# Gates of the last dense tile: from one-hot matmuls to scatters that add into cleared DRAM

## The chip, the cores and the metric

The kernel runs on one core of one Trainium2 chip. The metric is the time of one execution in microseconds (us) on the device; runs of the kernel before took 4015.42 to 4017.12 us, with a median of 4016.08 over 3 runs. A profile of one further execution comes with them.

## The reference, cut to what matters

The model is a backbone of two layers over 256 context tokens and 512 latent tokens of width 1024. Each layer has a mixer (layer 0: attention and a short convolution; layer 1: mLSTM) and then PEER, a mixture of 16384 tiny experts. For each token and each of 8 heads, PEER scores two sets of 128 keys, takes the best 16 of each, the best 16 of their sums, and a softmax over these:

```
cand = (s1[..., :, None] + s2[..., None, :]).reshape(PEER_BLOCK, PEER_HEADS, PEER_TOPK * PEER_TOPK)
cidx = (i1[..., :, None] * PEER_NKEYS + i2[..., None, :]).reshape(...)
top, pos = lax.top_k(cand, PEER_TOPK)
idx = jnp.take_along_axis(cidx, pos, axis=-1)
g = jax.nn.softmax(top, axis=-1)
ue, ve = u[idx], v[idx]
act = jax.nn.gelu(jnp.einsum('td,thkd->thk', xb, ue).astype(jnp.float32), approximate=False)
return jnp.einsum('thk,thkd->td', (g * act).astype(xb.dtype), ve)
```

So each token has 128 pairs of an expert's number and a gate. Two heads of one token can pick the same expert; their gates then add up. Layer 0 does this for 768 tokens (6 tiles of 128), layer 1 for the 512 latent ones (4 tiles).

## The kernel before, in words

PEER has two phases a layer. `peer_u` (L659) computes the activations of the experts, `peer_v0` (L1091) and `peer_v1` (L1151) multiply them by the gates and by v. Tokens are treated in two ways. The first `NG` tiles (2 in layer 0, 1 in layer 1) are *gathered*: GpSimd fetches the u rows of the chosen experts by indirect DMA, 128 rows of 4 KB each time (`dot`, L917), and VectorE takes the dot product (L923). All other tiles (4 and 3) are *dense*: TensorE multiplies them with all 16384 rows of u, in a loop of 128 steps c, each with 24 matmuls (8 blocks of the width, 3 products of the split float32, L676) over 512 columns in layer 0 and 384 in layer 1. A step's result goes through Gelu on ScalarE (`ga`, L1022) and to DRAM. Before each step ScalarE and VectorE split the next block of u into a high and a low part (`split_u`, uh and ul, with high priority). In steps 0 to 16 TensorE also projects the queries and VectorE takes the top 16 of the keys.

A dense tile needs its gates as a matrix over all experts and tokens. `stage2(t)` makes it. `cands`, `decode` and `soft` find the 128 expert numbers (two halves, idk) and gates of each token, for four heads at a time, on VectorE. `tr` transposes them on TensorE, `fin` makes 16-bit copies. Then, for every 8 tokens, `prep` (L857 to L860) makes one-hot matrices with 4 VectorE operations, and two `gbuild` (L874, L876) multiply them, 8 matmuls into one PSUM bank (gps), which ScalarE copies into `stg`. After 32 tokens four stores of 512 KB each (L756) put `stg` into the DRAM tile `gd`, laid out as [4, 128, 128, 32]: group of 32 tokens, first key, second key, token. The v phase loads it with `gf` (L1062).

What of this is done in which step is set by a planner at the end of `peer_u`. It has queues of items with a cost in us and the earliest step: `route` (heads of the gathered tiles), `one` (heads, prep and gbuild of the dense tiles), `dots` and `bgq` (modulation weights of the next layer). Each step is given a share (`given`) of the sum of all costs, in the ratio of its slack, and takes items from the queue that lies furthest behind its line (`lag`), which runs from the first to the second step in `goal`, until the share is spent. Instructions on one engine run in the order in which they stand in its queue, and so do the DMAs that SP, ScalarE and GpSimd issue. A DMA that depends on an earlier one waits on the issuing engine.

The first mixer (`mixer0`) loops over 8 heads of attention in units; the scores of a head run beside the weighted sum of the head before it.

Of the kernel before, what the change touches and what calls it, by code (L numbers as in the profile page):

```python
# [10 lines left out]
F32 = mybir.dt.float32  # L11
# [3 lines left out]
U32 = mybir.dt.uint32  # L15
AF = mybir.ActivationFunctionType
ALU = mybir.AluOpType
# [4 lines left out]
P = 128  # L22
# [23 lines left out]
TOPK = 16  # L46
# [14 lines left out]
GAB = 4  # L61

NG = (2, 1)
SEGS = ((0, NCTX), (NCTX, NLAT))


# [5 lines left out]
def kernel(ctx: ExitStack, tc: tile.TileContext, a: dict, out: bass.AP, dbg=None, stop=None):  # L72
    nc = tc.nc
# [6 lines left out]
    def mkpsum(st, name):  # L80
# [5 lines left out]
    tok = [a["tok"][t * P:(t + 1) * P, :] for t in range(NT)]  # L86
    gds = [[dram.tile([4, P, P, 32], F32, name=f"gd{v}_{t}") for t in range(n - NG[v])]
           for v, n in enumerate((NT, NLAT // P))]

    cv = const.tile([P, KD, 2], F32, name="cv")  # L90
    nc.sync.dma_start(cv, a["cvec"])
# [4 lines left out]
    ng = const.tile([P, 2, 2, KD], F32, name="ng")  # L96
# [118 lines left out]
    def mixer0(pk_open):  # L215
        with ExitStack() as st:
            rst = ExitStack()
            mcp = mkpool(st, "m0mc")
            mch = mcp.tile([P, 4, T], F32R, name="mch")
            mcl = mcp.tile([P, 4, T], F32R, name="mcl")  # L220
            m0b = mkpool(rst, "m0b", side="right")
            pqh = m0b.tile([P, 2, T], F32R, name="pqh")
# [234 lines left out]
            with ExitStack() as st2:  # L457
# [62 lines left out]
                for h in range(H0 + 1):  # L520
                    pts = {}
                    sc = scores(qks.pop(h), pts) if h < H0 else []
                    for u in range(8):
                        if u < len(sc):
                            sc[u]()
                        if u < len(prev):
                            prev[u]()
                        if u == 1 and 2 <= h + 1 < H0:
                            qks[h + 1] = prep(h + 1)
                    prev = attend(h, pts)  # L530
# [120 lines left out]
    def peer_u(layer, tiles):  # L651
# [8 lines left out]
        with ExitStack() as s1:  # L660
# [27 lines left out]
            pool.iota(c15, pattern=[[0, 4 * TOPK]], base=15, channel_multiplier=0)  # L688
            prev1 = up.tile([P, 4, TOPK + 1], F16, name="prev1", bufs=1)
            vec.memset(prev1, 0.0)  # L690
            urow = [up.tile([P, P], U32, name=f"urow{j}", bufs=1) for j in range(ng)]
            gact = [up.tile([P, P], F32, name=f"gact{j}", bufs=1) for j in range(ng)]
            sq = ExitStack()
# [67 lines left out]

            def stage2(t):
                H = 2 if t < ng else 4
                keep = t >= ng
                d = {}

                def cands(h0):
                    def f():
                        if h0 == 0:
                            d["g"] = up.tile([P, PH, TOPK], F32, name="g" if keep else f"g{t}", bufs=2 if keep else 1)  # L770
                            if keep:
                                d["id"] = up.tile([P, 2, PH, TOPK], F32, name="idk")
                        hs = slice(h0, h0 + H)
                        top = d["top"] = up.tile([P, H, TOPK], F32, name="top")
                        pos = d["pos"] = up.tile([P, H, TOPK], U32, name="pos")
                        vv = v16[t].rearrange("p (h q) k -> p h q k", q=2)[:, hs]
                        c = up.tile([P, H, 65], F32, name="cand", bufs=1)
                        for o, r0, rn, m in ((0, 0, 1, 16), (16, 1, 2, 8), (32, 3, 4, 4), (48, 7, 8, 2), (64, 15, 1, 1)):
                            vec.tensor_tensor(c[:, :, o:o + rn * m].rearrange("p h (r m) -> p h r m", m=m),
                                              vv[:, :, 0, r0:r0 + rn, None].to_broadcast([P, H, rn, m]),  # L780
                                              vv[:, :, 1, None, 0:m].to_broadcast([P, H, rn, m]), op=ALU.add)
                        for h in range(H):
                            w_ = up.tile([P, 65], F32, name="candw", bufs=1)
                            topk16(top[:, h, :], pos[:, h, :], c[:, h, :], w_)
                    return f

                def decode(h0):
                    def f():
# [12 lines left out]
                        vec.tensor_tensor(pt, ps_, pt, op=ALU.bitwise_and)  # L801
                        vec.tensor_copy(pq[:, 1], pt.rearrange("p (h k) -> p h k", k=TOPK))
                        if not keep:
                            d["t"] = up.tile([P, 2, H, TOPK], F32, name="idt")
                        dst = d["id"][:, :, h0:h0 + H] if keep else d["t"]
                        for q, (tab, op) in enumerate(((lo16, ALU.is_ge), (i16v, ALU.is_equal))):
                            eq = up.tile([P, H, TOPK, TOPK], F16, name="eq", bufs=1)
# [19 lines left out]
                def ids(h0):  # L827
                    ks = slice(h0 * TOPK, (h0 + H) * TOPK)
                    return ks, [d["t"][:, q].rearrange("p h k -> p (h k)") for q in range(2)]

                def tr():
                    tp = pp.tile([P, 512], F32, name="tp", bufs=2)
# [65 lines left out]

                def heads(h0):
                    need = 2 * (h0 + H) + 1  # L900
                    last = None if keep else rows(h0)
                    return [(cands(h0), 1.6 * H, need), (decode(h0), 0.7 + 1.4 * H, need), (soft(h0), 1.0, need)] + \
                        ([(last, 0.5, need)] if last else [])

# [38 lines left out]
                GP.extend((gp, io))  # L943

            qi = [q_items(hp) for hp in range(2 * PH)]
            st2 = [stage2(t) for t in range(n)]
            route = []
            for h0 in range(0, PH, 2):
                route += [x for t in range(ng) for x in st2[t][0](h0)] + [(found, 0.0, 0)]
            heads = [[x for h0 in (0, 4) for x in st2[t][0](h0)] + [(st2[t][1], 0.0, 0)] for t in range(ng, n)]  # L950
            one = heads[0]
            for t in range(ng, n):
                nxt = heads[t + 1 - ng] if t + 1 < n else []
                one.append((st2[t][2], 1.0, 0))
                for pf, g0, g1 in st2[t][3]:
                    one.append((pf, 2.75, 2 * PH + 1))
                    for gf in (g0, g1):
                        pend.append(gf)
                        if len(pend) > 3:
                            one.append((pend.pop(0), 0.0, 0))  # L960
                        if nxt:
                            one.append(nxt.pop(0))
                one += nxt
# [1 line left out]
            total_dots = P * ng  # L965
            dots = [(dot(x), 1.3, (x, 1)) for x in range(total_dots)] + [(st2[t][4], 0.3, (total_dots - 1, 1)) for t in range(ng)]
            bgq = [(f, 1.33 * (2 if layer == 0 and x < 24 else 1), 0) for x, f in enumerate(bg)]
            queues = [route, one, dots, bgq]
            goal = [(4, 18), (8, 118), (8, 125), (17, 124)]
            whole = [sum(x[1] for x in q) for q in queues]  # L970
            left = list(whole)
            slack = []
# [12 lines left out]
            def can(q, c):  # L985
                if not queues[q]:
                    return False
                need = queues[q][0][2]
                return need[0] < at["rows"] if isinstance(need, tuple) else need <= c or c == 127

            uhl, los = {}, {}

# [17 lines left out]
            for c in range(128):  # L1010
# [26 lines left out]
                while True:  # L1037
                    ok = [q for q in range(len(queues)) if can(q, c)]
                    if not ok or (spent > given and c < 127):
                        break  # L1040
                    q = max(ok, key=lambda q: lag(q, c))
                    f, w, _ = queues[q].pop(0)
                    with tc.issue_after(los[min(c + LAG, 127)]):
                        f()
                    left[q] -= w
                    spent += w
                if 1 <= c <= 2 * PH:
                    for f in qi[c - 1][3]:
                        f()
# [620 lines left out]
```

## Time and profile before

The profiled execution took 4018.06 us; its span from the first instruction to the last is 4015.8 us.

| engine | busy us | share of the span |
|---|---|---|
| TensorE, matmuls (PE) | 3754.6 | 93% |
| TensorE, weight loads (PEld) | 3208.5 | 80% |
| VectorE (DVE) | 3220.2 | 80% |
| ScalarE (ACT) | 1512.0 | 38% |
| GpSimd (POOL) | 1317.5 | 33% |

The DMA engines moved 1036.51 MB, 258 GB/s on the mean. The mean granted clock of TensorE is 0.970 of full speed.

A busy time is a sum over instructions that can overlap: a matmul's record lasts longer than the distance to the next. A wait is put down to what ended it. In the rows below, a number after x is a count, and what stands in brackets at a row's end is the idle time of that engine before it and what ended it. SPq and ACTq are the queues in which these engines issue DMAs. The DMA share is the mean busy share of the core's 16 DMA engines and can read above 1.

### The profile page before, as it was taken

The page shows a single profiled execution, that of the slowest core. Times are in us where ns is not written, and L with a number is a line of the kernel's source. Part 1 is how long each engine was busy: PE and PEld are TensorE (multiplying, and loading weights), DVE is VectorE, ACT ScalarE, POOL GpSimd, SP SyncE. Part 2 cuts the span into 40 slices and gives each one's busy share as a digit, 9 for nine tenths or more (in the row PEclk, how much of TensorE's full clock was granted, in tenths as well). Part 3 has the DMA queues.
Part 4 walks back from the last instruction along what each step waited for, and adds up shares of the span by engine and source line. Part 5 has one row for each costly group of instructions (what it writes and reads, how often), then busy time and mean ns, then how long its engine had stood idle before and what let it go on. Part 6 is the DMA issues. An engine that isn't in the chain of part 4 may idle for free. (4 is left out here: it accounts for less than half of the span.)

```text
span 4015.8 us, 54004 instructions
## 1 busy us (share of the span) xinstructions
PE 3754.6 (93%) x19201; PEld 3208.5 (80%) x19201; DVE 3220.2 (80%) x6734; ACT 1512.0 (38%) x2435; POOL 1317.5 (33%) x962
## 2 busy tenths in 40 slices
PE   6988989999999995999999899888999999899998
PEld 5776777877787774888888789867899999788887
DVE  7766699898899986988898854458897977588887
ACT  4355422333333332322222355542344443333333
POOL 2521201044434434767676312212012312232221
PEclk9999999999999997999999989989999999999999
DMA  7301443289899999999999721046368888899995
GB/s 244 103 6 50 159 154 130 100 307 342 303 351 333 371 366 357 389 390 388 391 388 390 266 70 44 18 170 219 107 226 291 313 294 301 316 387 360 359 357 213
DMA packets 411662, 1036.51 MB, mean 258 GB/s; under 512 B 35584, under 2 KB 170240, under 8 KB 411392
## 3 DMA queue, kind: packets, MB, share of 16 engines
q1 hardware_dynamic: 261920, 498.69, 35.7%
q0 software_dynamic: 114336, 416.34, 28.4%
q10 hardware_dynamic: 35136, 118.05, 7.5%
q8 instruction: 150, 2.46, 0.2%
q14 instruction: 120, 0.98, 0.1%
HBM read 906.05 MB, written 126.88 MB: 257 GB/s over the span
## 5 line engine op out<-in xcount | busy, mean ns | idle before, releaser
L917 POOL DMA_INDIRECT urows<-in_u_rows,urow x384 | 493.0, 1284 | 1243.6 <-DVE urows L923 847.6
L1080 POOL DMA_INDIRECT vrows<-in_v_t,vrow x384 | 601.8, 1567 | 581.0 <-DVE accg L1088 333.9
L676 PE MATMUL aps<-pnh,uh 128*128 128x512 f32 (+1 forms) x2048 | 766.0, 374 | 10.8 <-ACT ga L1022 7.1
L676 PE MATMUL aps<-pnh,ul 128*128 128x512 f32 (+1 forms) x2048 | 759.3, 371 | 2.9 <-DVE ul L111 2.9
L676 PE MATMUL aps<-pnl,uh 128*128 128x512 f32 (+1 forms) x2048 | 757.5, 370 | 0.0
L108 ACT CAST uh<-uf 128x1024 fp32r<-128x1024 f32 x256 | 269.2, 1052 | 725.9 <-PE aps L676 684.7
L923 DVE SCALAR_TENSOR_TENSOR urows<-urows,px 128x1024 f32<-128x1024 f32 x384 | 465.0, 1220 | 47.9 <-DMA urows<-in_u_rows,urow 46.8
L108 ACT CAST vh<-vf 128x1024 fp32r<-128x1024 f32 x256 | 269.2, 1052 | 552.5 <-issue 283.9
L676 PEld LDWEIGHTS aps<-pnh,uh 128*128 128x128 f32 x2048 | 389.9, 190 | 57.0 <-ACT ga L1022 9.6
L111 DVE TENSOR_TENSOR vl<-vf,vh 128x1024 fp32r<-128x1024 f32 x256 | 313.1, 1223 | 150.3 <-ACT vh L108 147.2
L676 PEld LDWEIGHTS aps<-pnh,ul 128*128 128x128 f32 x2048 | 387.9, 189 | 49.7 <-DVE ul L111 6.3
L676 PEld LDWEIGHTS aps<-pnl,uh 128*128 128x128 f32 x2048 | 388.8, 190 | 42.6
L111 DVE TENSOR_TENSOR ul<-uf,uh 128x1024 fp32r<-128x1024 f32 x256 | 312.7, 1222 | 102.9 <-ACT uh L108 100.6
L1111 PE MATMUL acc<-vh,vwh 128*128 128x512 f32 x1024 | 317.7, 392 | 48.4 <-ACT vwh L108 48.3
L1111 PE MATMUL acc<-vh,vwl 128*128 128x512 f32 x1024 | 316.8, 391 | 1.0 <-DVE vwl L111 1.0
L1111 PE MATMUL acc<-vl,vwh 128*128 128x512 f32 x1024 | 316.5, 390 | 0.0
L1088 DVE SCALAR_TENSOR_TENSOR vacc<-vrows,gw,vacc 128x1024 f32<-128x1024 f32 x254 | 314.3, 1281 | 0.0
L1111 PEld LDWEIGHTS acc<-vh,vwh 128*128 128x128 f32 x1024 | 193.2, 189 | 90.1 <-ACT vwh L108 50.1
L1176 PE MATMUL acc<-vh,vwh 128*128 128x512 f32 x768 | 238.4, 392 | 13.5 <-ACT vwh L108 12.9
L108 ACT CAST vwh<-gaf 128x512 fp32r<-128x512 f32 (+1 forms) x256 | 144.3, 564 | 277.5 <-DVE gaf L1069 178.5
L874 PE MATMUL gps<-p,p 128*128 128x128 f16 x1792 | 243.0, 296 | 4.9 <-DVE p L860 4.9
L1176 PE MATMUL acc<-vl,vwh 128*128 128x512 f32 x768 | 237.7, 391 | 0.0
(438 smaller groups left out, 7497.1 us busy)
## 6 DMA issues: line engine op xcount, KB each, us to landing
uf<-in_u_t SPq DMA_DIRECT2D x256, 512.0 KB
vf<-in_v_t SPq DMA_DIRECT2D x256, 512.0 KB
gd<-stg ACTq DMA_DIRECT2D x112, 512.0 KB
gf<-gd SPq DMA_DIRECT2D x224, 256.0 KB
wmt<-in_w_modT SPq DMA_DIRECT2D x90, 512.0 KB
gad<-ga ACTq DMA_DIRECT2D x64, 512.0 KB
gaf<-gad SPq DMA_DIRECT2D x64, 512.0 KB
gad<-ga ACTq DMA_DIRECT2D x64, 384.0 KB
```

The costliest lines, as they stand in the source:

```text
L108: act.copy(hi, src)
L111: return el.tensor_tensor(lo, src, hi.bitcast(F32), op=ALU.subtract)
L676: pe.matmul(ps[:, o:o + w], x[:, k, :], blk[q][:, k, :w], start=(k == 0 and x is wh and q == 0), stop=(k == KD - 1 and x is wl))
L874: pe.matmul(gp[:, i * P:(i + 1) * P], p1[:, g, :, i], p2[q][:, g, :, i], start=q == 0, stop=q == 1)
L917: nc.gpsimd.indirect_dma_start(out=r, out_offset=None, in_=a["u_rows"], in_offset=bass.IndirectOffsetOnAxis(ap=urow[j][:, k:k + 1], axis=0))
L923: vec.scalar_tensor_tensor(r, r, 1.0, PK["x"][j], op0=ALU.mult, op1=ALU.mult, accum_out=gact[j][:, k:k + 1])
L1080: nc.gpsimd.indirect_dma_start(out=r, out_offset=None, in_=a["v_t"].rearrange("l c k d -> (l c k) d"), in_offset=bass.IndirectOffsetOnAxis ...
L1088: vec.scalar_tensor_tensor(acc, r, gw[:, k:k + 1], acc, op0=ALU.mult, op1=ALU.add)
L1111: pe.matmul(acc[i][hf], x[:, ts_], y[:, hf * 512:(hf + 1) * 512], start=(c == 0 and first), stop=(c == 127 and end))
L1176: pe.matmul(acc[i][hf], x[:, ts_], y[:, hf * 512:(hf + 1) * 512], start=(c == 0 and first), stop=(c == 127 and last))
```

## The change

The last tile of each layer (`NSC = (1, 1)`) keeps its heads, but its gates no longer go through transposes, one-hot matrices, matmuls and stores. Instead its part of `gd` is cleared by 16 DMAs of 512 KB from a tile of zeros, one in each unit of the first mixer's attention from the second head on (32 for both layers, on SP's queue). `spots` turns each token's expert numbers into positions in `gd`, in `srow`, by two VectorE operations for each half of the heads. `scatter` then writes one column of `srow`: an indirect DMA on GpSimd's queue that adds 128 gates, one of each token and 4 bytes each, to 128 places in `gd`. There are 128 of them in a layer. They are sent between the items of the planner, after items with a cost above 1.0 us, along a line from step 8 to step 122; what is left goes out in step 125. The heads of the scattered tile get a queue of their own, `early`, with the steps 8 to 22 as its line, and the line of `one` begins at step 10 in place of 8. Three small tiles get three buffers.

```diff
+NSC = (1, 1)
+SC_END = 123
...
+    def clear(v, t, zero, x, n):
+        g = gds[v][t].rearrange("b p j t -> (b p j t)").rearrange("(x p y t) -> x p y t", x=n, p=P, t=P)
+        nc.sync.dma_start(g[x], zero[:, None, :].to_broadcast([P, P // n, P]))
...
+            zero = mcp.tile([P, P], F32, name="zero")
+            vec.memset(zero, 0.0)
+            wipe = [(v, len(gds[v]) - 1 - i, zero, x, 16) for v in range(2) for i in range(NSC[v]) for x in range(16)]
...
+                        if wipe and h:
+                            clear(*wipe.pop(0))
...
+            spos = up.tile([P, 1], F32, name="spos", bufs=1)
+            pu = up.tile([P, 2], U32, name="spu", bufs=1)
+            pool.iota(pu, pattern=[[0, 2]], base=0, channel_multiplier=1)
+            pf2 = up.tile([P, 2], F32, name="spf", bufs=1)
+            vec.tensor_scalar(pu[:, 0:1], pu[:, 0:1], 5, None, op0=ALU.logical_shift_right)
+            vec.tensor_scalar(pu[:, 1:2], pu[:, 1:2], 31, None, op0=ALU.bitwise_and)
+            vec.tensor_copy(pf2, pu)
+            vec.scalar_tensor_tensor(spos, pf2[:, 0:1], float(P * P * 32), pf2[:, 1:2], op0=ALU.mult, op1=ALU.add)
+            scat = list(range(n - NSC[layer], n))
+            srow = {t: up.tile([P, P], U32, name=f"srow{t}", bufs=1) for t in scat}
...
-                keep = t >= ng
+                keep = ng <= t < n - NSC[layer]
...
+                def spots(h0):
+                    def f():
+                        ks, (i0, i1) = ids(h0)
+                        rf = up.tile([P, 4 * TOPK], F32, name="rowf", bufs=1)
+                        vec.tensor_scalar(rf, i0, float(P * 32), spos[:, 0:1], op0=ALU.mult, op1=ALU.add)
+                        vec.scalar_tensor_tensor(srow[t][:, ks], i1, 32.0, rf, op0=ALU.mult, op1=ALU.add)
+                        gates[t] = d["g"].rearrange("p h k -> p (h k)")
+                        ready[t] += range(ks.start, ks.stop)
+                    return f
...
-                    last = None if keep else rows(h0)
+                    last = None if keep else rows(h0) if t < ng else spots(h0)
...
-            heads = [[x for h0 in (0, 4) for x in st2[t][0](h0)] + [(st2[t][1], 0.0, 0)] for t in range(ng, n)]
+            heads = [[x for h0 in (0, 4) for x in st2[t][0](h0)] + [(st2[t][1], 0.0, 0)] for t in range(ng, scat[0])]
+            early = [x for h0 in (0, 4) for t in scat for x in st2[t][0](h0)]
...
-            queues = [route, one, dots, bgq]
-            goal = [(4, 18), (8, 118), (8, 125), (17, 124)]
+            queues = [route, one, dots, bgq, early]
+            goal = [(4, 18), (10, 118), (8, 125), (17, 124), (8, 22)]
...
+            sent, due = 0, P * len(scat)
+
+            def scatter():
+                ts_ = [t for t in scat if ready[t]]
+                if not ts_:
+                    return 0
+                t = max(ts_, key=lambda x: len(ready[x]))
+                k = ready[t].pop(0)
+                nc.gpsimd.indirect_dma_start(
+                    out=gd[t - ng].rearrange("b p j (t o) -> (b p j t) o", o=1),
+                    out_offset=bass.IndirectOffsetOnAxis(ap=srow[t][:, k:k + 1], axis=0),
+                    in_=gates[t][:, k:k + 1], in_offset=None, compute_op=ALU.add)
+                return 1
...
+                    if w > 1.0 and sent * (SC_END - 9) < due * (c - 8):
+                        sent += scatter()
+                while c == 125 and scatter():
+                    sent += 1
```

## Rows read from the trace of the kernel before

**Rows 1.** Busy us of each engine by stretch; then granted clock, DMA share, GB/s.
```profile
475.00:760.00 285.00, 264.27 (x1389) 226.51 (x1390) 260.04 (x1140) 90.60 (x132) 15.71 (x13) 0.94 0.41 136
1100.00:1550.00 450.00, 440.27 (x2230) 348.75 (x2228) 409.36 (x728) 158.60 (x226) 181.44 (x136) 1.00 0.94 351
1600.00:2200.00 600.00, 600.00 (x2649) 496.94 (x2648) 533.30 (x558) 175.94 (x218) 412.00 (x229) 1.00 1.05 389
3010.00:3445.00 435.00, 435.00 (x2708) 425.69 (x2708) 347.32 (x580) 175.70 (x264) 111.78 (x91) 1.00 0.85 298
200.00:350.00 150.00, 133.42 (x732) 104.58 (x730) 111.12 (x245) 87.69 (x188) 42.86 (x27) 0.98 0.01 4
```

**Rows 2.** Groups by line, shapes apart: busy us, mean ns, idle time before.
```profile
L874 PE MATMUL gps<-p,p 128*128 128x128 f16 x1792 | 243.0, 296 | 4.9 <-DVE p L860 4.9
L860 DVE TENSOR_TENSOR p<-p2e,idT 128x1024 f16<-128x1024 f16 x224 | 148.3, 686 | 65.7 <-PE gps L874 63.7 <-PE aps L676 1.4 <-issue 0.6
L812 DVE TENSOR_REDUCE idk<-eq 128x64 f32<-128x1024 f16 x28 | 34.0, 1215 | 0.0
```

**Rows 3.** Chain of waits in layer 1: start, us, what.
```profile
3065.94 1.90 PE gps L874 x16
3067.84 4.25 PE aps L676 x24
```

**Rows 4.** TensorE in order of time, layer 0: start, us, instruction.
```profile
1517.80 1.82 PE L874 MATMUL gps<-p,p 128*128 128x128 f16 x14
1519.37 0.49 PE L676 MATMUL aps<-pnh,ul 128*128 128x512 f32 x1
```

**Rows 5.** The end of a layer's u phase, engines in order of time.
```profile
1593.75 1.22 PE L1111 MATMUL acc<-vh,vwh 128*128 128x512 f32 x2 [43.65 <-ACT vwh L108]
...
1575.21 1.22 DVE L923 SCALAR_TENSOR_TENSOR urows<-urows,px 128x1024 f32<-128x1024 f32 x1
...
1577.18 6.02 SPq L1062 DMA_DIRECT2D gf<-gd  x4
...
3452.31 0.38 SPq L1062 DMA_DIRECT2D gf<-gd  x1
```

**Rows 6.** A small VectorE operation like those added, in order of time.
```profile
1108.42 0.34 DVE L891 TENSOR_SCALAR rowf<-idt 128x32 f32<-128x32 f32 x1
```

**Rows 7.** DMA queues in 800 to 1500, then 1560 to 2200: packets, MB, share.
```profile
q10 hardware_dynamic: 15163, 55.23, 19.9%
...
q1 hardware_dynamic: 86273, 121.56, 53.9%
```

**Rows 8.** The next loads in SP's queue after the middle of attention.
```profile
368.39 10.45 SPq L579 DMA_DIRECT2D oht<-in_tok  x6
```

**Rows 9.** Gathers of u rows (L917) alone: GpSimd busy us, clock, DMA share.
```profile
760.00:1550.00 790.00, 315.46 (x239) 0.99 0.90 328
```

**Rows 10.** Gelu of steps 9 and 125: layer 0, then layer 1.
```profile
656.86 0.59 ACT L1022 ACTIVATE ga<-aps 128x512 f32<-128x512 f32 x1
1537.73 0.59 ACT L1022 ACTIVATE ga<-aps 128x512 f32<-128x512 f32 x1
2816.64 0.48 ACT L1022 ACTIVATE ga<-aps 128x384 f32<-128x384 f32 x1
3455.40 0.86 ACT L1022 ACTIVATE ga<-aps 128x384 f32<-128x384 f32 x2
```

**Rows 11.** Two gathers as issued, and the dots that waited for them.
```profile
2758.33 1.01 POOL L917 DMA_INDIRECT urows<-in_u_rows,urow  x1 [76.82 <-DVE rowf L891]
2762.81 1.27 DVE L923 SCALAR_TENSOR_TENSOR urows<-urows,px 128x1024 f32<-128x1024 f32 x1 [0.84 <-DMA urows<-in_u_rows,urow]
...
1551.77 1.98 POOL L917 DMA_INDIRECT urows<-in_u_rows,urow  x1 [0.30 <-issue]
1564.01 1.23 DVE L923 SCALAR_TENSOR_TENSOR urows<-urows,px 128x1024 f32<-128x1024 f32 x1 [1.76 <-DMA urows<-in_u_rows,urow]
```

**Rows 12.** Waits by line: us in total, times, longest.
```profile
DVE urows L923 <- DMA urows<-in_u_rows,urow: 46.8, 36, 3.4
```

More of the change, by code (lines that the diff above doesn't have):

```diff
@@ L773, in f @@
                         hs = slice(h0, h0 + H)
-                        top = d["top"] = up.tile([P, H, TOPK], F32, name="top")
-                        pos = d["pos"] = up.tile([P, H, TOPK], U32, name="pos")
+                        top = d["top"] = up.tile([P, H, TOPK], F32, name="top", bufs=3)
+                        pos = d["pos"] = up.tile([P, H, TOPK], U32, name="pos", bufs=3)
                         vv = v16[t].rearrange("p (h q) k -> p h q k", q=2)[:, hs]
@@ L803, in f @@
                         if not keep:
-                            d["t"] = up.tile([P, 2, H, TOPK], F32, name="idt")
+                            d["t"] = up.tile([P, 2, H, TOPK], F32, name="idt", bufs=3)
                         dst = d["id"][:, :, h0:h0 + H] if keep else d["t"]
@@ L945, in peer_u @@
             qi = [q_items(hp) for hp in range(2 * PH)]
+            ready, gates = {t: [] for t in scat}, {}
             st2 = [stage2(t) for t in range(n)]
@@ L949, in peer_u @@
                 route += [x for t in range(ng) for x in st2[t][0](h0)] + [(found, 0.0, 0)]
-            heads = [[x for h0 in (0, 4) for x in st2[t][0](h0)] + [(st2[t][1], 0.0, 0)] for t in range(ng, n)]
+            heads = [[x for h0 in (0, 4) for x in st2[t][0](h0)] + [(st2[t][1], 0.0, 0)] for t in range(ng, scat[0])]
+            early = [x for h0 in (0, 4) for t in scat for x in st2[t][0](h0)]
             one = heads[0]
-            for t in range(ng, n):
-                nxt = heads[t + 1 - ng] if t + 1 < n else []
+            for t in range(ng, scat[0]):
+                nxt = heads[t + 1 - ng] if t + 1 < scat[0] else []
                 one.append((st2[t][2], 1.0, 0))
```

## The prediction

> **What bounds it.** I read the busy time by stage first, since a share over the whole span averages stages with different limits [rows 1]. The change touches the two stages in which `peer_u` runs (about 475 to 1577 us in layer 0, 2690 to 3464 us in layer 1) and the attention of the first mixer. In the stretch 1100 to 1550 TensorE is busy 440 of 450 us, in 3010 to 3445 all 435 of 435. VectorE is next: 409 of 450 and 347 of 435. The DMA engines stand at 0.94 and 0.85. GpSimd is a third busy. In attention (200 to 350) the DMA engines do almost nothing, 0.01.
>
> The groups by line say what fills TensorE beside the products with u: the matmuls of `gbuild` (gps, L874), 1792 for seven dense tiles, so 256 for each tile [rows 2]. A busy time of pipelined matmuls overstates what leaving them out frees, so I take the price from the chain of waits, which covers layer 1: 16 of them stand there with 1.90 us, between steps of 24 products with 4.25 us, and nothing else is on the chain for hundreds of us [rows 3]. In layer 0 TensorE's order of time shows the same price: fourteen begin at 1517.80 and the next product at 1519.37, 0.112 us each, and that product is longer by 0.1 us, so 1.9 us for sixteen [rows 4].
>
> Layer 0 has one more bound. The first product with v starts at 1593.75, after 43.65 us without work for TensorE, so since 1550; meanwhile VectorE works off dots of gathered rows until 1576.4, and the load of gates follows at 1577.18 [rows 5]. So there the end is set by VectorE and the gathers, 26 us after TensorE.
>
> **What goes.** One dense tile in each layer loses 16 `prep`, 32 `gbuild`, `tr`, `fin` and 16 stores.
> TensorE: 16 x 1.90 = 30.4 us [rows 3, 4] and three transposes of about 0.2 us (an estimate from the 0.112 us of a gps matmul), 31 us a layer, all of it on TensorE's path in layer 1 and in layer 0 while TensorE is the bound.
> VectorE: 64 operations of 686 ns [rows 2], 44 us a layer (such times overlap a little, so I count 38 to 44), and `fin`. This is more than TensorE loses, so VectorE doesn't become the bound in TensorE's place, and the tail of dots in layer 0 can follow TensorE's 31 us.
> ScalarE: 32 evacuations, off the path.
>
> **What is added.** `spots` and its tables: per layer about eight VectorE operations like those of `rowf` and `urow`, 0.34 us or less each [rows 6], under 3 us, within the 38 to 44 that go. Cost 0; uncovered it is 3 us a layer.
>
> The heads of the scattered tile move from the middle to steps 8 to 22. The planner hands each step the same share of all work, so they push out other items (loads of modulation weights, dense heads) and add nothing to a step; the total of work is lower. VectorE is busy 260 of 285 us there and TensorE 264 [rows 1], so what isn't pushed out costs: at worst the 25 us of one tile's two halves on VectorE, an estimate from six operations of 0.7 to 1.2 us and some thirty of 0.2 us in each half, the sizes of [rows 2, 6]. I take 0.
>
> The clears: 32 DMAs of 512 KB on SP's queue in heads 1 to 4, in packets of 512 bytes. Such packets fill most of the first queue in 1560 to 2200: 86273 packets in 53.9% of 640 us on 16 engines, 64 ns each [rows 7]. 32 x 1024 / 16 x 64 ns = 131 us of the engines, from about 210 to 340. What is queued behind them on SP is the loads of oht, issued from 368 on [rows 8]. Hidden; if they ran over, the output projection would wait by as much, up to some 30 us. I take 0.
>
> The scatters: 128 a layer on GpSimd's queue. The trace has none. Three prices:
> (a) GpSimd's time, by the gathers, 315.46 / 239 = 1.32 us each: 169 us a layer. GpSimd had 790 - 315 and 435 - 112 us free in the two dense stretches [rows 1, 9]. Hidden.
> (b) The engines' time for 8 packets each. Least 0; by the 512-byte packets 8 x 64 ns = 0.5 us; by packets of 4 KB (15163 in 19.9% of 700 us, 147 ns) 1.2 us [rows 7]. I take 0.5, since the transfer is small: 66 us a layer, less the 19 us of the 16 stores that go. In layer 0 that is 0.90 x 790 = 711, + 47 = 758 us of work in 759 us, a share of 1.0; the stage after holds 1.05 for 600 us [rows 1, 9]. Just hidden.
> (c) The wait. All scatters of a tile add into one DRAM tile, so each waits on GpSimd for the landing of the one before, and the gathers of u rows behind it in the queue wait too, then the dots on VectorE, and behind those, in VectorE's order, the split of the next u block that TensorE needs. What counts is the time from one scatter to the next. Step 9 to step 125 is 657 to 1538 in layer 0 and 2817 to 3456 in layer 1 [rows 10]. Less 31 us, the budget is 850 / 128 = 6.6 us and 608 / 128 = 4.75 us. From below: the first gather of layer 1 is issued at 2758.33 and landed at 2762.81, 4.48 us for 512 KB; at the 389 GB/s that the engines moved in 1600 to 2200 [rows 1] 1.4 of that is data, so 3.1 us for a transfer with hardly any. From above: the gather issued at 1551.77, with four in flight and the engines full, landed at 1564.0, 12.2 us [rows 11]. I take 4.5 us, nearer the lower row: the gather that slips in behind a scatter moves its data while the next one waits for the landing, so there is seldom more than a part of one gather ahead. Under both budgets, in layer 1 by a hair. The Trainium skill ("DMA: Bandwidth & Descriptors", Anatomy of one DMA) gives a GpSimd transfer a fixed 2.0 us; the row shows 3.1. By the page a chain of 128 x 2.0 us would leave half of layer 1 free and the sum would be the one without the charge below.
>
> By the pacing rule the 128th scatter is due at step 122, so the first load of gates in layer 1, issued in step 126 (3452.31 [rows 5]), finds it landed.
>
> I charge the extra waits with 6 us: dots waited 46.8 us for 384 gathers [rows 12]; the same for 256 scatters is 31 us, and I let VectorE's idle time take four fifths.
>
> **Sum.** 2 x 31 = 62, less 6: 56 us off. The profiled execution took 4018.06 us (span 4015.8), the median of the runs is 4016.08, so 3960 from the median. Own range 3938 (no charge, the tail of layer 0 shrinks by VectorE's full 39 us and some DMA waits of its last 26 us) to 3975.
>
> **Rivals.**
> The chain of scatters becomes the bound of layer 1 and the kernel is slower. Place: GpSimd's queue, wait for the landing of the scatter before. Above 4.75 us a scatter, layer 1 lasts 128 times the difference longer; the whole gain is gone at 4.75 + 62 / 128 = 5.2 us. At 5.5 us it costs 96 us: 4016 - 62 + 96 = 4050. Layer 0 follows only above 6.6 us. For it: even the lone gather took 4.48 us [rows 11]. Against it: as the chain slows the gathers, the queue empties and the landing comes nearer to 3.1 us. The Trainium skill ("DMA: Bandwidth & Descriptors", Rules for kernel authors) says of an accumulating DMA that nothing holds its bytes between read and write and that the next must wait for the earlier one's semaphore; no run so far shows what that wait lasts.
> Between the two: a landing near 5.0 us binds in layer 1 only and returns its 31 us: 4016 - 62 + 32 = 3986.
> The engines fill up. With 1.2 us a scatter: layer 0 (711 - 19 + 154) / 1.05 = 806 us for 790, layer 1 (370 - 19 + 154) / 1.05 = 481 for 435, in all 4016 + 16 + 46 = 4078. For it: the shares of 0.94 and 0.85. Against it: the stores that go, and packets a thousandth of the size.
>
> **Chances.** Forecast 0.58; between 0.15; chain slower 0.17; engines full 0.05; the crossing of gain and loss by chance 0.05. Within 0.2% (8 us, about what a measurement of this kernel can tell from no change) is that last one. Faster: 0.58 + 0.15 = 0.73, same 0.05, slower 0.22. The range reaches from 3935 to 4035: it takes in all of the forecast but its lowest tail (0.03) and the slower case up to a landing of 5.4 us; outside stay 0.12 of the chain and 0.05 of the engines.
>
> **What would show it.** Right: 1280 gps matmuls and 80 stores of stg; steps of layer 1 still 4.25 us with 1.90 for gps and nothing between; GpSimd's waits on the scatter before it short, its dots seldom waiting for rows; layer 0 ending some 31 us earlier, with a tail of dots no longer than before. Wrong: TensorE waiting for the split of u in layer 1 while GpSimd waits on scatters; a DMA share over 1.05 in 1100 to 1520; the load of gates at the end of a layer waiting for a scatter; attention or the output projection after it longer than before.

## The result, and the profile after

The changed kernel takes 4446.99 us (median of 4 runs, 4443.15 to 4465.08), the kernel before 4015.75 beside it: a ratio of 1.108, 95% interval 1.1062 to 1.1097. It is 431 us slower where 56 us faster were forecast. The rival in which the chain of scatters becomes the bound has the right sign and place, but its 4050 us are far off too.

The head of the page after: busy time, share of the span, instructions.

```profile
span 4441.2 us, 53040 instructions
...
PE 3766.0 (85%) x18683; PEld 3210.9 (72%) x18683; DVE 3150.2 (71%) x6615; ACT 1473.3 (33%) x2369; POOL 1739.2 (39%) x1220
```

No engine has become the bound; they all wait more. Which of them waits first is read from the waits by line (us in total, times, longest), where [rows 12] had 46.8 us for the dots:

```profile
POOL gd L1032 <- DMA gd<-g,srow: 447.2, 198, 8.3
DVE urows L954 <- DMA urows<-in_u_rows,urow: 445.9, 142, 22.5
...
DVE gaf L1120 <- DMA gf<-gd: 179.3, 8, 111.5
...
PE aps L687 <- DVE ul L117: 176.6, 40, 21.8
...
PE acc L1162 <- ACT vwh L114: 118.3, 3, 113.7
```

Read as a chain: GpSimd waits for the scatter before (447 us), VectorE's dots wait for the gathers behind it in GpSimd's queue (446 us), and TensorE waits for the split of u that stands behind the dots (177 us). The third line and the last are a second loss, at the end of a layer: the gates can't be loaded until the last scatter has landed, and the first product with v waits for them.

Stretches of layer 0 with scatters, without, and at its end, then the same of layer 1 (busy us of each engine; at the end granted clock, DMA share, GB/s):

```profile
800.00:1150.00 350.00, 264.46 (x1067) 204.76 (x1066) 225.96 (x531) 85.86 (x112) 216.93 (x149) 0.86 0.72 221
1150.00:1400.00 250.00, 245.18 (x1186) 196.70 (x1185) 231.19 (x442) 83.93 (x116) 118.31 (x84) 1.00 0.95 354
1700.00:1815.00 115.00, 4.74 (x21) 3.49 (x19) 23.31 (x41) 2.86 (x5) 61.99 (x45) 0.54 0.55 166
3140.00:3440.00 300.00, 224.03 (x1197) 219.18 (x1196) 181.36 (x449) 86.30 (x118) 166.65 (x103) 0.87 0.62 184
3440.00:3600.00 160.00, 160.00 (x992) 157.00 (x991) 120.62 (x183) 61.94 (x94) 38.80 (x35) 1.00 0.84 304
3790.00:3900.00 110.00, 6.64 (x38) 6.32 (x36) 0.00 (x0) 0.98 (x2) 54.72 (x41) 0.55 0.22 39
```

TensorE is busy all 160 of 160 us where no scatter stands in the queue and 224 of 300 where they do. There are stretches without any, which a pace of one a step excludes: the addresses come twice a layer, and the second time late. These are the instructions of `spots` that write them, on VectorE in order of time (start, us), for layer 0 and 1:

```profile
813.62 0.21 DVE L857 SCALAR_TENSOR_TENSOR srow<-idt,rowf 128x64 uint32<-128x64 f32 x1
...
1460.32 0.21 DVE L857 SCALAR_TENSOR_TENSOR srow<-idt,rowf 128x64 uint32<-128x64 f32 x1
...
3138.22 0.21 DVE L857 SCALAR_TENSOR_TENSOR srow<-idt,rowf 128x64 uint32<-128x64 f32 x1
...
3614.31 0.22 DVE L857 SCALAR_TENSOR_TENSOR srow<-idt,rowf 128x64 uint32<-128x64 f32 x1
```

Following the planner's rule with its own costs gives the steps: 22 and 98 in layer 0, 21 and 102 in layer 1. After its first half the queue `early` stays 14 us behind its line, and its second half waits until no other queue is further behind. The first 64 scatters of layer 0 run from 815.5 to 1144, the others from 1460.8 to 1795.8; in layer 1 the planner leaves 24 for step 125.

The end of layer 1, engines in order of time, which answers to [rows 5]: the last two scatters, the load that waits for them, VectorE and TensorE.

```profile
3883.10 1.55 POOL L1032 DMA_INDIRECT gd<-g,srow  x1 [1.73 <-DMA gd<-g,srow]
3886.45 1.55 POOL L1032 DMA_INDIRECT gd<-g,srow  x1 [1.80 <-DMA gd<-g,srow]
...
3889.51 0.38 SPq L1113 DMA_DIRECT2D gf<-gd  x1
...
3900.25 0.56 DVE L1120 TENSOR_TENSOR gaf<-gaf,gf 128x384 f32<-128x384 f32 x1 [111.54 <-DMA gf<-gd]
...
3901.40 1.22 PE L1227 MATMUL acc<-vh,vwh 128*128 128x512 f32 x2 [104.76 <-ACT vwh L114]
```

Nothing else runs here, and still a scatter follows the last by 3.3 us: 1.55 of GpSimd, 1.7 to 1.8 of waiting. TensorE stands still for 104.76 us, and for 113.69 at the end of layer 0, where it was 43.65 before.

### The profile page after: what moved, and what is told of

The parts are those of the page before. It is cut to its first block, busy times and chain, and to the rows that moved or that the text cites. A ratio compares the mean times of both kernels' runs of the same rounds, so it can differ in the third digit from the quotient of the medians.

```text
span 4441.2 us, 53040 instructions
## 1 busy us (share of the span) xinstructions
PE 3766.0 (85%) x18683; PEld 3210.9 (72%) x18683; DVE 3150.2 (71%) x6615; ACT 1473.3 (33%) x2369; POOL 1739.2 (39%) x1220
## 3 DMA queue, kind: packets, MB, share of 16 engines
q0 software_dynamic: 151200, 416.48, 28.4%
## 5 line engine op out<-in xcount | busy, mean ns | idle before, releaser
L687 PE MATMUL aps<-pnh,ul 128*128 128x512 f32 (+1 forms) x2048 | 789.7, 386 | 176.6 <-DVE ul L117 176.6
L1131 POOL DMA_INDIRECT vrows<-in_v_t,vrow x384 | 577.1, 1503 | 598.5 <-DVE accg L1139 336.4
L687 PE MATMUL aps<-pnh,uh 128*128 128x512 f32 (+1 forms) x2048 | 787.9, 385 | 6.3 <-ACT px L219 4.1
L954 DVE SCALAR_TENSOR_TENSOR urows<-urows,px 128x1024 f32<-128x1024 f32 x384 | 465.7, 1220 | 446.3 <-DMA urows<-in_u_rows,urow 445.9
L687 PE MATMUL aps<-pnl,uh 128*128 128x512 f32 (+1 forms) x2048 | 781.1, 381 | 0.0
L1032 POOL DMA_INDIRECT gd<-g,srow x256 | 454.3, 1775 | 600.3 <-DMA gd<-g,srow 447.2
L687 PEld LDWEIGHTS aps<-pnh,ul 128*128 128x128 f32 x2048 | 406.6, 199 | 239.2 <-DVE ul L117 193.0
L687 PEld LDWEIGHTS aps<-pnh,uh 128*128 128x128 f32 x2048 | 408.2, 199 | 53.7 <-ACT px L219 4.7
L687 PEld LDWEIGHTS aps<-pnl,uh 128*128 128x128 f32 x2048 | 405.5, 198 | 46.9
L1162 PE MATMUL acc<-vl,vwh 128*128 128x512 f32 x1024 | 316.3, 390 | 0.0
L1120 DVE TENSOR_TENSOR gaf<-gaf,gf 128x512 f32<-128x512 f32 (+1 forms) x256 | 157.8, 616 | 186.6 <-DMA gf<-gd 179.3
## 6 DMA issues: line engine op xcount, KB each, us to landing
gaf<-gad SPq DMA_DIRECT2D x64, 512.0 KB, 12.4
```

Source lines behind the costliest of these rows:

```text
L687: pe.matmul(ps[:, o:o + w], x[:, k, :], blk[q][:, k, :w], start=(k == 0 and x is wh and q == 0), stop=(k == KD - 1 and x is wl))
L954: vec.scalar_tensor_tensor(r, r, 1.0, PK["x"][j], op0=ALU.mult, op1=ALU.mult, accum_out=gact[j][:, k:k + 1])
L1032: nc.gpsimd.indirect_dma_start(out=gd[t - ng].rearrange("b p j (t o) -> (b p j t) o", o=1), out_offset=bass.IndirectOffsetOnAxis(ap=srow[t ...
L1120: vec.tensor_tensor(w3, w3, st["gf"][:, :, c % 4, :], op=ALU.mult)
L1131: nc.gpsimd.indirect_dma_start(out=r, out_offset=None, in_=a["v_t"].rearrange("l c k d -> (l c k) d"), in_offset=bass.IndirectOffsetOnAxis ...
L1162: pe.matmul(acc[i][hf], x[:, ts_], y[:, hf * 512:(hf + 1) * 512], start=(c == 0 and first), stop=(c == 127 and end))
```

## The experiments

In all of them the clears and the other tiles stay. Times are medians; each ratio is to the kernel before on the same chip. Where the scatters go into spare tiles or are left out, the gates of one tile in each layer stay zero.

| kernel | us | ratio (95%) |
|---|---|---|
| changed kernel | 4446.99 | 1.108 (1.1062 to 1.1097) |
| no scatter | 3962.43 | 0.9865 (0.9848 to 0.9881) |
| early | 4351.53 | 1.0835 (1.0816 to 1.0853) |
| no wait | 4263.08 | 1.0626 (1.0606 to 1.0646) |
| early, no wait | 4180.86 | 1.0409 (1.0392 to 1.0426) |
| early, pinned | 4229.85 | 1.0521 (1.0503 to 1.0539) |
| late, pinned | 4418.88 | 1.0986 (1.0967 to 1.1004) |
| early, pinned, no wait | 4024.39 | 1.0007 (0.9996 to 1.0018) |
| early, no scatter | 3955.14 | 0.9839 (0.9822 to 0.9855) |
| early, pinned, two chains | 4035.64 | 1.0046 (1.003 to 1.0062) |
| early, pinned, iota | 3951.57 | 0.9827 (0.981 to 0.9843) |
| early, pinned, plain write | 4138.49 | 1.0296 (1.0266 to 1.0326) |
| early, pinned, plain, no wait | 3978.35 | 0.9895 (0.9877 to 0.9913) |

**First four: what is removed, when, and the wait.**

```
# no scatter: in scatter(), ahead of the DMA
+                return 1
# early: the planner takes the new queue first
-                    q = max(ok, key=lambda q: lag(q, c))
+                    q = max(ok, key=lambda q: (q == 4, lag(q, c)))
# no wait: eight spare tiles in turn
-                    out=gd[t - ng].rearrange("b p j (t o) -> (b p j t) o", o=1),
+                    out=spare[k % 8].rearrange("b p j (t o) -> (b p j t) o", o=1),
```

No scatter. 

> Issues no scatter at all; ranks, addresses, clears and the order of everything else stay as in the changed kernel, so the gates of one tile in each layer stay zero. It isolates what the change removes and its small additions. If the prediction's term of removal is right (31 us of TensorE in each layer, the clears and the moved heads at nothing): 3954 us, give or take 15. If the clears, the moved heads or something else in the change cost what the result lost: 4150 us or more. Every theory on the scatters themselves expects the first.

3962.43 us: the removal pays what was forecast, and clears and heads cost next to nothing. All of the loss is in the scatters.

Early. 

> The planner takes the heads of the scattered tile ahead of all other items, so both halves are ready by step 20 (layer 0) and 23 (layer 1) and the scatters go out at about one a step to step 122. Nothing else is changed. Theory A (bunching: the second half of the ranks came only at steps 98 and 102, so 64 scatters had to go in some 25 steps, several a step, and the rest drained at the layer's end; one wait by itself fits in a step): most of the 487 us between forecast and result comes back, 3970 to 4050 us, no drain of TensorE at the layer's end beyond that of before. Theory B (the wait is too long at any pace: each scatter holds GpSimd's queue until the one before has landed, 4.6 to 5.0 us from scatter to scatter, and with the gathers and their dots behind it that doesn't fit in a step): TensorE still waits for the split of u all along, 4250 us or more. In layer 1, with 4.6 us of scatter and some 4.75 us of step, theory B may hold alone: then about 4100.

4351.53: theory A gets 95 us of its 400, and theory B's 4250 or more holds. The end of the layer is free of scatters now, but TensorE's wait for the split of u has grown from 177 to 291 us:

```profile
PE aps L687 <- DVE ul L117: 291.5, 37, 72.5
```

No wait. 

> The scatters keep their number, their places in the order and their data, but go in turn into eight spare DRAM tiles, so that a scatter waits only for the one eight places before it; the gates of the tile stay zero. Theory A and theory B both put the loss on the wait for the scatter just before: 3955 to 4010 us here, with GpSimd at 1.55 us for each scatter and nothing between. Theory C (the loss is in the scatters' own work: GpSimd's time to write descriptors, or small packets on the DMA engines that slow the loads of u and the gathers): 4300 us or more, as in the changed kernel.

Early, no wait. 

> Both edits at once: heads of the scattered tile first, and the scatters in turn into eight spare DRAM tiles (the gates of the tile stay zero). Its distance from the early version is the cost of the wait at an even pace; its distance from the version without scatters is the cost of issuing them and of their traffic. Theory A: within 40 us of the early version. Theory B: 200 us or more under it. Both expect it within 30 us of the version without scatters (3955 to 3985); theory C expects it 200 us or more above that.

4263.08 and 4180.86: both A and B are too low by 200 us or more, though hardly any scatter waits for another. Theory C comes nearer, but the trace shows something else. In order of time in layer 1 of the last one, GpSimd first, then VectorE and TensorE (the number in brackets is the idle time before):

```profile
2871.55 0.94 POOL L950 DMA_INDIRECT urows<-in_u_rows,urow  x1 [0.31 <-DVE tkw L660]
2933.51 1.64 POOL L1034 DMA_INDIRECT spare<-g,srow  x1 [61.02 <-DVE v L661]
2935.45 1.57 POOL L1034 DMA_INDIRECT spare<-g,srow  x1 [0.30 <-issue]
...
3188.39 1.23 DVE L956 SCALAR_TENSOR_TENSOR urows<-urows,px 128x1024 f32<-128x1024 f32 x1 [138.86 <-DMA urows<-in_u_rows,urow]
...
3191.93 0.69 PE L689 MATMUL aps<-pnh,ul 128*128 128x384 f32 x1 [136.76 <-DVE ul L119]
```

From 2933.51 on all 128 scatters of the layer stand in one block, to 3182.2, and the 24th gather comes behind them. The code issues about one a step; the queue doesn't have them so. A gather follows the dot that frees its buffer, and the dots are tied to the step (`issue_after`, which ties only what runs on VectorE); a scatter is tied to nothing but its addresses, so in laying out GpSimd's queue it comes as soon as these are there. In the trace of the early version the longest blocks without a gather between have 53 scatters in layer 0 and 43 in layer 1. This made a theory D: the order of the queue.

**Next three: the order of the queue.** The edit gives each scatter an edge to the instruction before it on GpSimd, in the order of the code.

```
-                nc.gpsimd.indirect_dma_start(
+                tc.keep_in_program_order(nc.gpsimd.indirect_dma_start(
...
```

Early, pinned. 

> The early version with one thing more: each scatter is pinned in GpSimd's queue behind the instruction that the program issues before it, so that scatters and gathers alternate as the steps issue them. In the early version and in the one without waits the queue didn't: nothing tied a scatter to its step, and blocks of 54 (layer 0) and 44 (layer 1) scatters stood in front of gathers whose dots VectorE, and behind it TensorE, waited for. Theory D (the order of GpSimd's queue: the loss is the blocks, whatever a scatter waits): 3960 to 4020 us, TensorE's waits for the split of u under 60 us in all (291 us in the early version). Theory B (a scatter waits 3 to 5 us for the one before and that alone is too much for a step): 4150 us or more.

Late, pinned. 

> The changed kernel with the pin alone; the second half of the ranks still comes at steps 98 and 102, so its 64 scatters are traced in some 25 steps, with 18 (layer 0) and 39 (layer 1) of them behind the last gather. Theory D: the first half costs nothing any more, the drain at the end of each layer (some 110 and 120 us without TensorE) stays: 4150 to 4250 us. Theory A without D (bunching in the program's order is all): no change from 4447. Theory B: 4300 us or more.

Early, pinned, no wait. 

> Early, pinned, and the scatters in turn into eight spare DRAM tiles (the gates of the tile stay zero), so that no scatter waits for the one before. Against the early pinned version it gives the price of the wait when the queue is in order; against the version without scatters (3962 us) the price of 256 scatters themselves. Theory D: 3960 to 3990, within 30 us of the early pinned version. Theory B: the same 3960 to 3990, but 150 us or more under it. Theory C (issue and traffic of the scatters cost by themselves): 4100 us or more here too.

4229.85, 4418.88 and 4024.39. The block costs 122 us with the wait (4351.53 to 4229.85) and 156 without (4180.86 to 4024.39), so D is real; but with the queue in order the wait costs 205 us more than none. That is theory B, and D alone falls; 4024 is still 34 us above what both expected without the wait. The end of the layer is not in the 205 us: TensorE's gap before the first product with v in layer 0 is 43.3 us with the wait and 42.2 without. The pin alone gives 28 us of 4447, under theory D's 200 to 300; 35 scatters of layer 1 and 16 of layer 0 still come behind the last gather there. GpSimd of the early pinned version in layer 0, in order of time:

```profile
1100.81 1.85 POOL L1032 DMA_INDIRECT gd<-g,srow  x1 [4.14 <-DMA gd<-g,srow]
1102.97 1.42 POOL L948 DMA_INDIRECT urows<-in_u_rows,urow  x1 [0.30 <-DVE p L891]
1104.69 0.94 POOL L948 DMA_INDIRECT urows<-in_u_rows,urow  x1 [0.30 <-DVE urows L954]
1105.93 1.95 POOL L1032 DMA_INDIRECT gd<-g,srow  x1 [0.30 <-issue]
1108.18 1.51 POOL L948 DMA_INDIRECT urows<-in_u_rows,urow  x1 [0.30 <-issue]
1110.00 0.94 POOL L948 DMA_INDIRECT urows<-in_u_rows,urow  x1 [0.30 <-issue]
1114.44 1.62 POOL L1032 DMA_INDIRECT gd<-g,srow  x1 [3.50 <-DMA gd<-g,srow]
```

Two gathers stand between two scatters, and still the scatter of 1105.93 keeps the next from starting until 1114.44, 8.5 us later: GpSimd sits idle 3.50 us, with the next gathers behind it.

**Last five: what the wait hangs on, and what is left without it.** "Two chains" is `spare[k % 2]`; "iota" puts `pool.iota(busy, pattern=[[1, 416]], ...)` in the place of the DMA; "plain" leaves out `compute_op=ALU.add`.

Early, no scatter. 

> No scatters, and the heads of the scattered tile ahead of all else as in the early versions (the gates of the tile stay zero). Against the version without scatters and with late heads (3962 us) it gives the price of moving the heads early. The prediction took 0, at worst 25 us a layer: 3955 to 3970 if that 0 holds; 3990 to 4020 if the early heads are what the pinned version without waits (4024) still loses.

3955.14: the early heads cost nothing, as the prediction took.

Early, pinned, two chains. 

> As the early pinned version, but the scatters go in turn into two spare DRAM tiles (the gates of the tile stay zero), so each waits for the one but last. In the pinned version a scatter landed some 3 to 7 us after its issue and a step of layer 1 has 4.75 us. If the wait costs only where a landing is longer than the distance of two scatters, two chains halve the need and nearly all of the 205 us between one chain (4230) and eight (4024) comes back: 4025 to 4060. If any wait on a DMA in GpSimd's queue costs, whatever its length, about half comes back: 4110 to 4150.

4035.64: 194 of the 205 us come back with one scatter's distance more. GpSimd's waits for scatters, with one chain and with two (us in total, times, longest):

```profile
POOL gd L1032 <- DMA gd<-g,srow: 460.0, 190, 7.6
...
POOL spare L1034 <- DMA spare<-g,srow: 62.3, 43, 5.6
```

The scatters by tile, with min, median and max from issue to landing (counted from the start of GpSimd's instruction, over those whose landing the trace has), in the two-chain version and then in the early one without pin and wait, where they stand in a block with little else in flight:

```profile
L1034 POOL DMA_INDIRECT spare<-g,srow x256: 1545/1727/2907, 680.2 to 3454.4; - x128
...
DMA to landing us min/median/max: 3.0/6.2/14.8
```

```profile
L1034 POOL DMA_INDIRECT spare<-g,srow x256: 1549/1559/2627, 680.9 to 3182.2; - x128
...
DMA to landing us min/median/max: 2.9/3.1/7.0
```

And the same with one chain, in the early pinned version, for layer 0 and then for layer 1:

```profile
L1032 POOL DMA_INDIRECT gd<-g,srow x128: 1552/1802/2722, 678.7 to 1638.4; - x128
...
DMA to landing us min/median/max: 3.0/5.7/12.4
...
L1032 POOL DMA_INDIRECT gd<-g,srow x128: 1545/1615/2619, 2941.6 to 3647.5; - x128
...
DMA to landing us min/median/max: 2.9/4.3/8.8
```

A scatter lands in 3.1 us by itself and in 6.2 us among gathers and loads at full pace (6.5 in layer 0, 5.3 in layer 1); with one chain, which slows the rest, in 5.7 and 4.3. From the first scatter to the last, one follows another with one chain by 7.6 us in layer 0 and 5.6 in layer 1, with two by 7.1 and 4.5. So one chain doesn't hold the pace and two nearly do. But the medians with one chain lie under the 6.6 and 4.75 us that a scatter has in the prediction, and still both layers lose. Why, the runs do not show; the landings spread from 2.9 to 12.4 us, and once the addresses are there ten or eleven scatters stand in a row.

Early, pinned, iota. 

> As the early pinned version, but in the place of each scatter GpSimd writes a row of numbers, 416 columns into a small tile, some 1.5 us, without any transfer (the gates of the tile stay zero). It has GpSimd's time of a scatter without its packets and without a wait. If what is left at eight chains (4024 against 3962) is GpSimd's time in front of the gathers: 4000 to 4025. If it is the traffic of the small packets: within 15 us of the version of early heads without scatters.

3951.57, but the stand-in was too short: a row of numbers took GpSimd 0.49 us, not 1.5.

```profile
L1033 POOL IOTA busy<- x256: 477/492/508, 639.2 to 3374.6; 128x416 f16 x128
```

So half a microsecond of GpSimd for each scatter is free; that its whole time is free, 1.91 us on the mean with eight chains, isn't shown. The 69 us that eight chains still lose against no scatters (4024.39 and 3955.14) can lie in that time or in the transfers. In layer 1 the trace points to GpSimd. The stretch from 3000 to 3300 without scatters, with iota, with eight chains of the plain writes that come below, and with eight chains of adding ones:

```profile
3000.00:3300.00 300.00, 298.99 (x1812) 294.29 (x1812) 234.08 (x387) 119.35 (x174) 86.98 (x70) 1.00 0.86 304
...
3000.00:3300.00 300.00, 300.00 (x1820) 295.61 (x1819) 234.35 (x391) 119.77 (x175) 136.06 (x155) 1.00 0.85 305
...
3000.00:3300.00 300.00, 296.33 (x1765) 290.50 (x1764) 231.89 (x417) 116.90 (x170) 194.04 (x151) 0.99 0.85 291
...
3000.00:3300.00 300.00, 282.36 (x1637) 277.34 (x1636) 226.25 (x425) 108.08 (x155) 250.17 (x151) 0.97 0.90 279
```

In the last row GpSimd is busy 250 us, and the 0.3 us between its instructions, 151 times, fill 45 of the other 50: it is the bound there, while a gather lands no later than without scatters (median 7.0 and 7.5 us).

Early, pinned, plain write. 

> As the early pinned version, but the scatters write instead of adding (a gate that falls on another of the same token replaces it). One chain, same waits, same order. If the wait is that of any small indirect transfer: 4215 to 4245, as with adding. If reading and adding in DRAM is what makes the landing long: 4150 or less.

Early, pinned, plain, no wait. 

> Early, pinned, scatters that write instead of adding, in turn into eight spare DRAM tiles (the gates of the tile stay zero). With eight chains the adding scatters cost 62 to 70 us though nothing waits for them, and GpSimd's time alone cost nothing. An adding scatter makes 144 packets, a writing one 32, by the packet counts of the first queue. If the rest is the DMA engines' time for these packets: 3960 to 3985, most of the 70 us back. If it is the scatter's place among the gathers whatever it moves: 4010 to 4030, as with adding.

4138.49 and 3978.35. Of the 69 us, 46 go with the adding; but a plain write also takes GpSimd less, 1.34 us on the mean for 1.91, so this doesn't separate GpSimd's time from the packets. With one chain, writing is 91 us faster than adding, of which 46 are these; GpSimd's waits for scatters fall only from 460.0 to 421.3 us. GpSimd's DMA queue of four versions (packets, MB, share of 16 engines over the span): no scatters (span 3951.6 us), adding with eight chains (4035.5), writing with eight chains (3983.5).

```profile
q0 software_dynamic: 114336, 416.34, 28.6%
```

```profile
q0 software_dynamic: 151200, 416.48, 30.4%
```

```profile
q0 software_dynamic: 122528, 416.48, 28.7%
```

An adding scatter makes (151200 - 114336) / 256 = 144 packets, a writing one 32. In time of the engines that is (30.4% of 4035.5 - 28.6% of 3951.6) / 256 = 0.38 us and 0.05 us each.

No version here beats the kernel before with all the gates in place: even with nothing waiting, adding scatters only equal it. Two chains whose tiles are both loaded and added in the v phase were not tried; they start from 4035.64 and add 8 MB of loads a layer.

## Why the prediction was wrong

**The step that failed** is part (c), the wait: "I take 4.5 us", "Under both budgets, in layer 1 by a hair", and with it "by the pacing rule the 128th scatter is due at step 122". It came to a charge of 6 us. Three things in it were wrong, and the runs price each; with 69 us that eight chains still lose they add up from 3955 without scatters to 4447, a sum that hangs on the order in which the steps are taken:

- The wait was taken as free because one landing fits in the mean time that a scatter has, and that comparison failed. Both bounds of the landing were right: the lower, 3.1 us, is the landing with little else in flight, the upper was 12.2. The 4.5 was about what one chain shows (5.7 in layer 0 and 4.3 in layer 1 where the order is kept, 3.7 over both in the changed kernel). These are under the budgets of 6.6 and 4.75 us, and yet 190 of 256 scatters waited, 460 us in all, and the chain costs 205 us. Of the 194 between two chains and one (4035.64 to 4229.85), 133 lie in layer 1 and 58 in layer 0: from the last product of v of layer 0 to the first of layer 1 it takes 1298 us with one chain and 1165 with two, and layer 0 starts v at 1667.0 and 1608.9. What in the chain makes it cost more than the medians say stays open.
- The queue was taken to follow the code. The prediction named what is queued behind a scatter, but not that nothing holds the scatter to its step: blocks, 122 us.
- The pace was taken from the scatters' own rule (step 9 to 125) without asking when their addresses come. They came in two batches, at 22 and 98, 21 and 102; the rule then catches up, 3 to 5 a step in layer 0, up to 3 in layer 1, and the rest drains at the layer's end. So the second 64 have some 25 steps; in layer 1 that is 23 of 608 / 116 = 5.2 us, or 1.9 us each, less than even the lower bound. That costs 95 us without the pin (4446.99 to 4351.53) and 189 with it (4418.88 to 4229.85).

TensorE's idle stretches cost twice: the granted clock is 0.54 in the drain of layer 0, near the lower of its two levels (1.2 GHz of 2.4), and 0.86 in the stretches where TensorE keeps waiting, against 1.00 where it doesn't. The same 18683 matmuls take 3766.0 us of TensorE here and 3698.7 without scatters.

**(b), the engines**: 0.5 us a scatter taken, 0.38 measured, so the size was about right, though the 64 ns for a packet of 512 bytes is a mean over packets of 1.4 KB (121.56 MB in 86273 of [rows 7]). "Just hidden" is not confirmed. In the profiled executions, eight chains end layer 0 55 us later than no scatters (first product with v at 1623.5 against 1568.5), and layer 1 takes 27 us more. In layer 1 GpSimd is full; in layer 0, where the DMA share in 1000 to 1500 is 0.95 with and without scatters and GpSimd has idle time left, the engines' time can be the cause (128 x 0.38 = 49 us), but plain writes with 0.05 us each lose 24 us there too, and no run isolates it. The Trainium skill ("DMA: Bandwidth & Descriptors", Rules for kernel authors) says of many small transfers that they should be joined, since under 64 KB one pays mostly overhead; the trace agrees, with 0.38 us for 512 bytes.

**The charge** of 6 us by VectorE's idle time fell with (c): dots waited 445.9 us, not 46.8 and 31.

**What held.** The removal: 3955 to 3962 us without scatters against 3954 from 62 us, layer 1 shorter by 33 us (31 forecast) and layer 0 by 22 (first v at 1571.8 for 1593.75). Spots and early heads cost 0. The clears are hidden but for some 3 us, though they ran from 59 to 190 us and not from 210 on: in 60 to 190 TensorE is busy 106.2 us for 109.1, and the first product with u starts at 479.1 for 475.6. The counts are the forecast ones, as the group of gps in the changed kernel shows (least, median and most ns of one, first and last start):

```profile
L905 PE MATMUL gps<-p,p x1280: 277/297/331, 966.9 to 3779.0; 128*128 128x128 f16 x183
```

**(a), GpSimd's time**, held only in part: a scatter takes 1.78 us on the mean in the changed kernel and 1.91 with eight chains, not 1.32, and that is hidden only while the scatters are spread; where some 1.4 come in a step of layer 1, GpSimd is full.

**The rivals.** The chain as the bound was the right mechanism, at 0.17 the second likeliest. Its price went with the difference of landing and step in layer 1 alone, 0.75 us at 5.5. Layer 1's own landing of 4.3 us with one chain would give nothing by the same formula, and the 5.3 us of two chains 4016 - 62 + 70 = 4024; 4230 was measured with the queue in order and the addresses early, and layer 0 lost too, under its 6.6 us. "Engines full" took 1.2 us each for a measured 0.38; that eight chains lose the gain even so may be GpSimd's time as much as the engines'.

## What to carry to other kernels

A chain of dependent small DMAs isn't free because its median landing fits in the time that each has: 4.3 us of 4.75 and 5.7 of 6.6 lost 194 us here, and a second target, which halves that chain, gave them back. Before pricing a paced DMA, look at when its addresses come and at what ties it to its step in the queue that issues it: if nothing does, it comes to stand in front of what other engines need. A wait in the queue of an idle engine reaches the bound engine through an engine in between that works in order. And an instruction that stands in for another has to take as long: 0.49 us in the place of 1.9 left GpSimd's time untested.

## What the runs showed of the hardware

An indirect scatter that adds 128 values of 4 bytes into DRAM takes GpSimd 1.56 to 1.73 us (medians of versions), one that writes them 1.13 to 1.18; it makes 144 packets against 32, and 0.38 us against 0.05 of 16 DMA engines with eight chains. Chained and alone, one follows another by 3.3 us. The Trainium skill ("DMA: Bandwidth & Descriptors", Anatomy of one DMA) gives a GpSimd transfer a fixed 2.0 us; no landing of an adding scatter here was under 2.9, and the median under load was 6.2 with two chains.
